# A gating mixer's norm: gamma and beta taken behind the spatial product

## The chip, the cores and the metric

The kernel runs on one core of a Trainium2 chip. The time is the device time of one execution in microseconds (us); the version before takes 566.77 us, the median of 3 runs (566.43 to 567.15). The engines have short names here, as in the profile: PE is the matrix engine (PEld its weight loads), DVE the vector engine, ACT the scalar engine, POOL the GpSimd engine, SP the engine that issues nearly all DMAs. Each engine takes its own instructions strictly in the order in which they were issued, and waits for the others by semaphores.

## The reference

A trunk of two layers over 256 tokens of width 1024. Layer 0 mixes tokens with a gated MLP, layer 1 with attention; each is followed by a gated FFN with a short convolution, and each sub-layer by a residual and a LayerNorm. Only the mixer of layer 0 changes:

```python
def chunked_gmlp(x, w_in, ln_g, ln_b, w_s, b_s, w_out):
    z = gelu(x @ w_in)
    u, v = split(z, 2)                       # 1024 columns each
    v = layer_norm(v, ln_g, ln_b)            # (v - mean) * rstd * gamma + beta, per token
    v = v.reshape(B, 2, 128, 8, 128)         # 2 chunks of 128 tokens, 8 groups of 128 channels
    w = tril(w_s)                            # per group a 128 x 128 causal matrix
    sv = einsum('gts,bnsgc->bntgc', w, v) + b_s.T[..., None]
    return (u * sv.reshape(B, S, 1024)) @ w_out
```

All data are float32. Gamma and beta differ per channel c; the weights w mix the tokens s of a chunk; b_s is one number per group and token t. Since the spatial product sums over tokens and gamma does not depend on them, sum over s of w[t,s] (n[s,c] gamma[c] + beta[c]) = gamma[c] (w n)[t,c] + beta[c] (sum over s of w[t,s]), where n is the normalized v.

## The kernel before, in words

Every large matrix product is made from three: operands are split into a high part (rounded to a faster 4-byte type) and a low remainder, and high x high, high x low and low x high are summed in PSUM. The weights come in chunks of 1 MB (`stream`, 128 x 2048 in the two tiles `raw`). For each half of a chunk ACT rounds the high part (`whi<-raw`, line 353) and DVE subtracts it to get the low one (`wlo<-raw,whi`, line 359); ten pairs `whi`/`wlo` are in use in turn. A chunk is loaded when the chunk five places ahead of it has been used. Chunks 0 to 3 are `a_v` (the columns of w_in for v), 4 to 7 `a_u` (for u), 8 to 11 `a_out`, then `f_up0` and so on. Chunk 4 lands in the tile that later holds x, hence `x<-in_a_u` and `wlo<-x,whi`.

The mixer, `gmlp` (lines 696 to 755), goes through four stages on PE:

1. v = x @ a_v, token-major: two token tiles t, each of two PSUM banks of 512 columns, eight steps k of the contraction.
2. For each of 8 groups g of u, channel-major: `cols_apart` with 16 matmuls (8 steps, a 512-column one with `whi` and a 256-column one with `wlo`); ACT copies half of the bank (`uparts<-bank`), DVE adds the other (`ff<-bank,uparts`), ACT applies the GELU.
3. Meanwhile v gets its GELU (ACT, `ff<-bank`), its statistics (`stats`, DVE: `BATCH_NORM_STATS2`, aggregate, add of epsilon; POOL: a power of -1/2 on one column, line 557) and its norm (`scaled`): per token tile two instructions of 512 columns, (v - mean) * gamma, and four of 256, (. * rstd) + beta, with gamma and beta as rows in the tile `lnrow`, copied to all partitions by a DMA.
4. `spatial(g)`: PE multiplies v's group with the masked weights `ws` into a PSUM half bank (`twos<-ff`, plain float32), DVE adds the bias row of the group (`ff<-twos,ff`), multiplies by u (`ff<-ff`), and the product is split into high (ACT, `rr<-ff`) and low (DVE, `rr<-ff,rr`). Then a_out contracts over the groups, k = g.

`load_mixer` loads the transposed spatial weights (`wsT`), masks them on POOL (`affine_select`, line 496) and loads the bias rows (`bs`). `load_rest` loads x again in token layout, `lncol` (gammas and betas as columns, for later norms) and the convolution's constants (`convc`).

The order of instructions on each engine is not the order of the code. Everything is recorded in a `Plan` with an estimated duration; `Plan.emit` (lines 124 to 220) walks through time with these estimates and picks on each engine the waiting operation with the earliest due time. PE's bulk matmuls keep their order, the `fill` ones (spatial products, transposes) slip in when they are estimated to be ready. What comes out is a fixed sequence per engine; a row that waits on the chip holds up everything behind it on its engine. `after` (line 76) only holds an issue back until a named one has been issued.

## Time and profile before

| | |
|---|---|
| median of 3 runs | 566.77 us (566.43 to 567.15) |
| the profiled execution's own time | 566.5 us |
| its span in the trace | 564.7 us |
| PE busy | 555.1 us, 98% of the span |
| DVE busy | 467.9 us, 83% |
| ACT busy | 363.9 us, 64% |
| POOL busy | 11.2 us, 2% (18 instructions) |
| mean granted PE clock | 0.996 |

The span runs from the first instruction to the last; 1.8 us of the execution lie outside it. In rows of the timeline the first number is the start in us from the span's start, the second the time from the first to the last instruction of the row, then engine, line, operation, output<-inputs by the program's names, shapes and a count; in brackets how long the engine had been idle before and what released it. "PE bank L341 <- DVE rr L359" in the list of waits reads: PE's instruction of line 341 that writes a PSUM bank waited for DVE's instruction of line 359 that writes `rr`; then total us, count, longest. Rows of a table of windows give, for a stretch of the span, the busy us and the count of instructions of PE, PEld, DVE, ACT and POOL, the granted clock (1.00 is full), the DMA engines' share and GB/s.

### The profile page before, as it was taken

How to read it: one execution, taken by the hardware profiler on the slowest of the kernel's cores; microseconds unless marked ns; L12 is line 12 of the kernel's file. 1: busy time of each engine (PE TensorE's matmuls, PEld its weight loads, DVE VectorE, ACT ScalarE, POOL GpSimd, SP SyncE). 2: the span in 40 equal slices, each digit the busy share in tenths (PEclk: the TensorE clock that was granted, in tenths of full speed). 3: DMA queues.
4: the chain of work that ended last, by engine and by line, in shares of the span. 5: the costliest groups of instructions: out<-in, count | busy, mean ns of one | idle time of the engine just before them, and what ended most of it. 6: DMA issues, size and time to landing. Idle time of an engine off the chain costs nothing.

```text
span 564.7 us, 8191 instructions
## 1 busy us (share of the span) xinstructions
PE 555.1 (98%) x3041; PEld 472.8 (84%) x3041; DVE 467.9 (83%) x886; ACT 363.9 (64%) x660; POOL 11.2 (2%) x18
## 2 busy tenths in 40 slices
PE   8999999999999999999999999999999999999994
PEld 6888788888888888888888887788888888888884
DVE  6599989999999897568868888589998999997426
ACT  6557568767777684535678888288777776885200
POOL 0010010000000000001000000000000000000001
PEclk9999999999999999999999999999999999999998
DMA  8977536454545559671655553506456455667202
GB/s 304 386 288 272 195 135 225 169 203 171 203 176 199 178 202 334 236 261 34 242 199 187 187 192 146 224 9 237 187 199 257 157 209 168 223 225 265 103 0 75
DMA packets 19856, 110.97 MB, mean 197 GB/s; under 512 B 2326, under 2 KB 5608, under 8 KB 7656
## 3 DMA queue, kind: packets, MB, share of 16 engines
q1 hardware_dynamic: 19672, 110.18, 54.0%
q8 instruction: 24, 0.39, 0.3%
q10 hardware_dynamic: 144, 0.26, 0.1%
q14 instruction: 16, 0.13, 0.1%
HBM read 109.36 MB, written 1.07 MB: 196 GB/s over the span
## 4 chain that ended last, share of the span: by engine, by line
PE 93%; DVE 5%; DMA 1%; issue 1%; ACT 0%; DVEq 0%
PE twos L341 52%; PE bank L341 38%; DVE wlo L359 2%; PE bank L347 1%; PE twos L347 1%; DMA raw<-in_a_out 1%; PE twos L974 1%; DVE ff L359 1%; DVE stat L551 1%; DVE ff L363 0%; DVE x L363 0%; DVE rr L359 0%; ACT whi L353 0%; ACT ff L353 0%; DVE stat L554 0%
## 5 line engine op out<-in xcount | busy, mean ns | idle before, releaser
L359 DVE TENSOR_TENSOR wlo<-raw,whi 128x1024 fp32r<-128x1024 f32 (+1 forms) x210 | 227.0, 1102 | 35.3 <-ACT whi L353 34.9
L353 ACT ACTIVATE whi<-raw 128x1024 fp32r<-128x1024 f32 (+1 forms) x210 | 193.7, 954 | 61.9 <-DMA raw<-in_f_dn 23.4
L341 PE MATMUL twos<-xt,whi 128*128 128x512 f32 x640 | 222.2, 394 | 0.0
L341 PE MATMUL twos<-xt,wlo 128*128 128x256 f32 x640 | 177.3, 277 | 0.0
L341 PEld LDWEIGHTS twos<-xt,whi 128*128 128x128 f32 x640 | 120.0, 188 | 27.8
L341 PE MATMUL bank<-whi,rr 128*128 128x512 f32 x432 | 135.7, 391 | 0.5 <-DVE rr L359 0.5
L341 PEld LDWEIGHTS twos<-xt,wlo 128*128 128x128 f32 x640 | 120.1, 188 | 0.1
L341 PEld LDWEIGHTS bank<-whi,rr 128*128 128x128 f32 x432 | 81.0, 188 | 18.2 <-DVE rr L359 0.9
L341 PE MATMUL bank<-wlo,rr 128*128 128x512 f32 x216 | 84.1, 389 | 0.0
L363 DVE SCALAR_TENSOR_TENSOR ff<-ff,convc 128x255 f32<-128x255 f32 (+1 forms) x160 | 70.3, 477 | 1.1 <-ACT ff L353 0.9
L341 PE MATMUL bank<-xt,whi 128*128 128x512 f32 x192 | 69.0, 401 | 0.0
L341 PE MATMUL bank<-xt,wlo 128*128 128x256 f32 x192 | 53.8, 280 | 0.0
L353 ACT ACTIVATE ff<-twos 128x512 f32<-128x512 f32 (+1 forms) x56 | 30.8, 565 | 33.6 <-PE twos L341 30.8
L353 ACT ACTIVATE ff<-ff,convc 128x256 f32<-128x256 f32 x80 | 46.5, 593 | 3.1 <-DVE ff L359 2.6
L341 PEld LDWEIGHTS bank<-wlo,rr 128*128 128x128 f32 x216 | 40.6, 188 | 8.1
L341 PEld LDWEIGHTS bank<-xt,whi 128*128 128x128 f32 x192 | 36.1, 188 | 8.8 <-issue 0.5
L341 PE MATMUL twos<-whi,xt 128*128 128x512 f32 x128 | 42.1, 396 | 0.0
L359 DVE TENSOR_TENSOR ff<-twos,ff 128x512 f32<-128x512 f32 (+1 forms) x48 | 30.7, 642 | 8.9 <-ACT ff L353 8.5
L341 PEld LDWEIGHTS bank<-xt,wlo 128*128 128x128 f32 x192 | 36.3, 189 | 0.1
L353 ACT ACTIVATE ff<-bank,lncol 128x128 f32<-128x128 f32 x48 | 18.8, 460 | 25.9 <-PE bank L347 25.8
L341 PEld LDWEIGHTS twos<-whi,xt 128*128 128x128 f32 x128 | 24.1, 188 | 4.7
L363 DVE SCALAR_TENSOR_TENSOR x<-x,bank 128x512 f32<-128x512 f32 x16 | 10.9, 684 | 20.6 <-PE bank L341 20.6
(86 smaller groups left out, 499.7 us busy)
## 6 DMA issues: line engine op xcount, KB each, us to landing
raw<-in_f_up SPq DMA_DIRECT2D x44, 1024.0 KB, 4.8
raw<-in_f_dn SPq DMA_DIRECT2D x22, 1024.0 KB, 4.9
raw<-in_b_qk SPq DMA_DIRECT2D x8, 1024.0 KB, 4.8
lnrow<-in_lnrow SPq DMA_DIRECT2D x5, 1024.0 KB, 6.1
raw<-in_a_out SPq DMA_DIRECT2D x4, 1024.0 KB, 5.1
raw<-in_b_v SPq DMA_DIRECT2D x4, 1024.0 KB, 4.8
raw<-in_b_o SPq DMA_DIRECT2D x4, 1024.0 KB, 5.0
raw<-in_a_v SPq DMA_DIRECT2D x7, 512.0 KB, 5.6
```

Source lines behind the costliest of these rows:

```text
L341: nc.tensor.matmul(o, l, x, start=start, stop=stop)
L347: nc.tensor.transpose(o, x, ident.ap)
L353: return plan.op("act", ns, lambda: nc.scalar.activation(o, x, func, **kw), r, w, table=table)
L359: dve(70 + 1.04 * flat(x), lambda: nc.vector.tensor_tensor(o, x, y, op=op), r, w)
L363: lambda: nc.vector.scalar_tensor_tensor(o, x, s, y, op0=op0, op1=op1), r, w)
L551: dve(70 + 1.04 * n, lambda j=j, o=o, n=n: nc.vector.bn_stats(s[:, j, :], x[:, o:o + n]), [(r, range(o // S, (o + n) // S))], [(st, [("st" ...
L974: nc.tensor.matmul(banks[-1], zeros[:, :P], zeros, start=True, stop=True)
```

## The change

v is only normalized, (v - mean) * rstd, by two `tensor_scalar` instructions of 512 columns per token tile. The rows gamma and beta of this norm are no longer loaded. Behind the spatial product a `scalar_tensor_tensor` takes the place of the addition: product times gamma (a column of `lncol`, which gains 16 columns) plus a table per group. This table, `bs`, is the bias plus beta[c] times the row sum of the masked weights, and is built on the chip:

- the spatial weights are loaded a second time, untransposed (`ws`, 0.5 MB), into the first half of the one tile that rotates through `lnrow`; POOL masks them; DVE sums over s (`tensor_reduce`, 128 x 1024 to 128 x 8);
- a DMA writes the 4 KB of sums to a scratch in DRAM, a second one reads them back to all 128 partitions (0.5 MB into the tile's second half);
- POOL multiplies, group by group, the sums (every eighth element) by beta's column, and adds the result to the bias rows: 16 instructions of 128 columns.

`lncol` is loaded in `load_mixer` now. The core of the diff:

```diff
     def load_mixer():
         wsT, bs = place("ff", 3072, SUB), place("ff", 4096, SUB)
+        natural = rowring.new()
+        nv = natural.ap[:, :SUB].rearrange("p (g s) -> p g s", g=GROUPS)
+        load(nv, a["ws"], [(natural, ["ws"])]).after = loads[5]
         load(wsT.ap, a["wsT"], [wsT])
+        load(lncol.ap, a["lncol"], [lncol])
         v = wsT.ap.rearrange("p (g t) -> p g t", g=GROUPS)
         plan.op("pool", 1100, lambda: nc.gpsimd.affine_select(
             v, v, pattern=[[0, GROUPS], [1, P]], compare_op=ALU.is_ge, fill=0.0, base=0,
             channel_multiplier=-1), [wsT], [wsT])
-        load(bs.ap, bass.AP(tensor=a["bs"].tensor, offset=a["bs"].offset, ap=[[0, P], [1, GROUPS * P]]), [bs])
-        return (wsT, v), (bs, bs.ap.rearrange("p (g t) -> p g t", g=GROUPS))
+        bv = bs.ap.rearrange("p (g t) -> p g t", g=GROUPS)
+        load(bs.ap, bass.AP(tensor=a["bs"].tensor, offset=a["bs"].offset, ap=[[0, P], [1, GROUPS * P]]),
+             [(bs, QUART), (bs, range(4, GROUPS))])
+        plan.op("pool", 1600, lambda: nc.gpsimd.affine_select(
+            nv, nv, pattern=[[0, GROUPS], [-1, P]], compare_op=ALU.is_ge, fill=0.0, base=0,
+            channel_multiplier=1), [(natural, ["ws"])], [(natural, ["ws"])])
+        sums, scr = Buf(sb.tile([P, GROUPS], F32, name="sums")), Buf(dram.tile([P, GROUPS], F32, name="sumscr"))
+        dve(1140, lambda: nc.vector.tensor_reduce(out=sums.ap, in_=nv, axis=mybir.AxisListType.X, op=ALU.add),
+            [(natural, ["ws"])], [sums])
+        load(scr.ap, sums.ap, [scr], [sums], nbytes=4096)
+        everywhere = natural.ap[:, SUB:]
+        load(everywhere, bass.AP(tensor=scr.ap.tensor, offset=scr.ap.offset, ap=[[0, P], [1, GROUPS * P]]),
+             [(natural, ["sums"])], [scr])
+        ev = everywhere.rearrange("p (t g) -> p g t", g=GROUPS)
+        for g in range(GROUPS):
+            plan.op("pool", 500, lambda g=g: nc.gpsimd.tensor_scalar_mul(
+                ev[:, g, :], ev[:, g, :], lncol.ap[:, 7 * KT + g:7 * KT + g + 1]),
+                [(natural, ["sums"]), lncol], [(natural, [g])])
+            plan.op("pool", 600, lambda g=g: nc.gpsimd.tensor_tensor(
+                bv[:, g, :], ev[:, g, :], bv[:, g, :], op=ALU.add), [(natural, [g]), (bs, [g])], [(bs, [g])])
+        return (wsT, v), (bs, bv)
...
             if (k, t) == (3, NT - 1):
-                rows = ln_rows(0)
                 ws, bs = load_mixer()
...
-                scaled(vt, vt.ap, st, mean, rstd, rows)
+                for o in (0, HALF):
+                    parts = range(o // S, (o + HALF) // S)
+                    ts(vt.ap[:, o:o + HALF], vt.ap[:, o:o + HALF], mean, rstd, ALU.subtract, ALU.mult,
+                       [(vt, parts), (st, ["mv", "rstd"])], [(vt, parts)])
...
-            tt(y3, b.ap[:, :S].rearrange("p (c t) -> p c t", c=NT), bs[1][:, g:g + 1, :].to_broadcast([P, NT, P]),
-               ALU.add, [b, bs[0]], [y])
+            stt(y3, b.ap[:, :S].rearrange("p (c t) -> p c t", c=NT), lncol.ap[:, 6 * KT + g:6 * KT + g + 1],
+                bs[1][:, g:g + 1, :].to_broadcast([P, NT, P]), ALU.mult, ALU.add, [b, (bs[0], [g]), lncol], [y])
```

The planner sees other operations and other estimates, so sequences move on every engine. In the rows below a name is a tile and its number, `[waits ...]` the semaphores, by engine or DMA queue, on which the row waits.

On DVE, at the passage from v's product to u's (raw_85, raw_86 and x are weight chunks, whi/wlo their high and low halves; stat holds the norm's statistics, lnrow_89 the untransposed spatial weights). Before:

```order
L359 TENSOR_TENSOR wlo_82<-raw_86,whi_72 128x1024 [waits DMAHW3_49,Activation_49]
L551 BN_STATS stat_90<-ff 128x6 [waits Activation_49]
L359 TENSOR_TENSOR wlo_83<-x,whi_73 128x1024 [waits DMAHW4_49]
L359 TENSOR_TENSOR wlo_84<-x,whi_74 128x1024 [waits Activation_49]
L359 TENSOR_TENSOR wlo_75<-raw_85,whi_65 128x1024 [waits DVE_49,DMAHW5_49,PE_49,Activation_49]
```

And now:

```order
L359 TENSOR_TENSOR wlo_82<-raw_86,whi_72 128x1024 [waits DMAHW3_49,Activation_49]
L510 TENSOR_REDUCE sums<-lnrow_89 128x8 [waits Pool_49]
L573 BN_STATS stat_90<-ff 128x6 [waits Activation_49]
L359 TENSOR_TENSOR wlo_83<-x,whi_73 128x1024 [waits DMAHW5_49]
L359 TENSOR_TENSOR wlo_84<-x,whi_74 128x1024 [waits Activation_49]
```

The sum over the weights stands between wlo_82 and the first statistics, ahead of the low halves of u's first chunk, and waits for POOL.

On SP, the DMA issues of the same stretch (sumscr is the scratch in DRAM). Before:

```order
L377 DMA x<-in_a_u 128x2048 [waits DMAHW4_49]
L377 DMA raw_85<-in_a_u 128x2048 [waits DMAHW1_49,DMAHW0_49,DVE_49]
L377 DMA lnrow_89<-in_lnrow 128x2048
L377 DMA ff<-in_wsT 128x1024 [waits DMAHW7_49]
L377 DMA ff<-in_bs 128x1024
L377 DMA lncol<-in_lncol 128x48
L377 DMA raw_86<-in_a_u 128x2048 [waits DMAHW3_49,DMAHW2_49,DVE_49]
L377 DMA raw_85<-in_a_u 128x2048 [waits DMAHW5_49,DVE_49]
```

And now:

```order
L377 DMA ff<-in_wsT 128x1024 [waits DMAHW4_49]
L377 DMA x<-in_a_u 128x2048
L377 DMA raw_85<-in_a_u 128x2048 [waits DMAHW1_49,DMAHW0_49,DVE_49]
L377 DMA lnrow_89<-in_ws 128x1024 [waits DMAHW7_49]
L377 DMA sumscr<-sums 128x8 [waits DVE_49]
L377 DMA ff<-in_bs 128x1024
L377 DMA lncol<-in_lncol 128x64 [waits DMAHW2_49]
L377 DMA convc<-in_convc 128x352 [waits DMAHW3_49]
L377 DMA raw_86<-in_a_u 128x2048 [waits DMAHW4_49,Activation_49]
L377 DMA raw_85<-in_a_u 128x2048 [waits DMAHW6_49,DMAHW5_49,DVE_49]
L377 DMA lnrow_89<-sumscr 128x1024 [waits DMAHW0_49]
```

wsT has moved ahead of u's first chunk, the 1 MB of gamma and beta is replaced by the 0.5 MB of untransposed weights, and the write of the sums, which waits for DVE, stands ahead of the bias and of u's third and fourth chunk (the last two raw rows).

On DVE, at the first spatial product (twos is its PSUM half bank, bank the one of u):

```order
L359 TENSOR_TENSOR wlo_80<-raw_85,whi_70 128x1024 [waits Activation_49]
L359 TENSOR_TENSOR ff<-bank_108,uparts_116 128x256 [waits Activation_49]
L363 SCALAR_TENSOR_TENSOR ff<-twos_104,lncol,ff 128x256 [waits DMAHW1_49,DMAHW2_49,PE_49,Pool_49]
L366 TENSOR_SCALAR ff<-ff,stat_90 128x512
L359 TENSOR_TENSOR ff<-ff 128x256 [waits DVE_49]
L366 TENSOR_SCALAR ff<-ff,stat_91 128x512
```

Before, the addition that stood in the place of the third row waited for at most one DMA queue and PE, and none of them for POOL; now each of the eight also waits for the POOL addition that completes its group's table.

More of the change, by code (lines that the diff above doesn't have):

```diff
@@ L450, in trunk_kernel @@
     ident, nhalf = const("ident", P), const("nhalf", 1)
-    lncol, convc = const("lncol", 6 * KT), const("convc", DEPTH * 2 * FT * 4)
+    lncol, convc = const("lncol", 8 * KT), const("convc", DEPTH * 2 * FT * 4)
     plan.op("pool", 400, lambda: make_identity(nc, ident.ap), (), [ident])
@@ L486, in ln_rows @@
         src = a["lnrow"]
-        o = load(b.ap, bass.AP(tensor=src.tensor, offset=src.offset + i * 2 * D, ap=[[0, P], [1, 2 * D]]), [b])
-        if i == 0:
-            o.after = loads[5]
+        load(b.ap, bass.AP(tensor=src.tensor, offset=src.offset + i * 2 * D, ap=[[0, P], [1, 2 * D]]), [b])
         return b, b.ap.rearrange("p (a d) -> p a d", a=2)
@@ L504, in load_rest @@
             load(xtok[t].ap, a["x"][:, t, :], [(xtok[t], QUART)])
-        load(lncol.ap, a["lncol"], [lncol])
         load(convc.ap, a["convc"], [convc])
@@ L577, in ln_back @@
         step = KT // len(waits)
-        lc = lncol.ap.rearrange("p (i a k) -> p i a k", i=3, a=2)
+        lc = lncol.ap.rearrange("p (i a k) -> p i a k", i=4, a=2)
         x = r.ap
@@ L1011, in _layout @@
         "b_o": by_rows(np.asarray(i["b_w_o"])[0]),
+        "ws": f(np.asarray(i["a_w_s"])[0].transpose(1, 0, 2)),
         "wsT": f(np.asarray(i["a_w_s"])[0].transpose(2, 0, 1).reshape(P, -1)),
@@ L1027, in _layout @@
     g["lnrow"] = f(np.stack([np.stack(p) for p in lns]))
-    g["lncol"] = f(np.stack([np.stack(p) for p in lns[1:4]]).reshape(3 * 2 * KT, P).T)
+    g["lncol"] = f(np.stack([np.stack(p) for p in lns[1:4] + lns[:1]]).reshape(4 * 2 * KT, P).T)
     cw, cb = np.asarray(i["f_conv_w"]), np.asarray(i["f_conv_b"])
```

## The prediction

> **What bounds the kernel now.** I read the page's totals and its chain first, then PE's list of waits, then the table of windows over the mixer, then the timeline of each engine there.
>
> ```profile
> PE 555.1 (98%) x3041; PEld 472.8 (84%) x3041; DVE 467.9 (83%) x886; ACT 363.9 (64%) x660; POOL 11.2 (2%) x18
> PE 93%; DVE 5%; DMA 1%; issue 1%; ACT 0%; DVEq 0%
> ...
> PE twos L974 <- DVE nhalf L453: 1.5, 1, 1.5
> PE bank L341 <- DVE rr L359: 0.5, 1, 0.5
> ...
> 30.00:40.00 10.00, 9.86 (x59) 8.56 (x58) 10.00 (x19) 5.67 (x9) 1.71 (x2) 1.00 0.73 247
> 40.00:50.00 10.00, 10.00 (x63) 8.93 (x63) 9.89 (x17) 6.41 (x11) 0.00 (x0) 1.00 0.66 248
> 50.00:60.00 10.00, 10.00 (x56) 8.61 (x55) 10.00 (x25) 7.35 (x14) 0.00 (x0) 1.00 0.71 270
> 60.00:70.00 10.00, 9.50 (x43) 7.53 (x42) 9.31 (x17) 4.81 (x10) 0.00 (x0) 1.00 0.62 216
> ```
>
> PE is the bound, and in the whole span it waits for another engine twice: 1.5 us at the start, 0.5 us once in a_out. Two things follow. The change adds and removes no work on PE, so at best it gains that half microsecond. And every new wait of PE stays in the time, since no later wait exists that could take it up. But in the mixer (30 to 64 us) DVE is full (fourth and fifth numbers of the windows: DVE's 10.00, 9.89, 10.00), and the 0.5 us is DVE being late. So two questions decide: does the change make PE wait where it did not, and does DVE come out earlier or later at the end of the mixer?
>
> **First place: the sum over the weights.** These rows give the passage from v to u.
>
> ```profile
> 13.46 0.42 SPq L377 DMA_DIRECT2D x<-in_a_u  x1
> 17.26 0.33 SPq L377 DMA_DIRECT2D raw<-in_a_u  x1
> 17.64 0.43 SPq L377 DMA_DIRECT2D lnrow<-in_lnrow  x1
> 18.11 0.44 SPq L377 DMA_DIRECT2D ff<-in_wsT  x1
> 20.96 0.33 SPq L377 DMA_DIRECT2D raw<-in_a_u  x1
> ...
> 21.05 1.06 ACT L353 ACTIVATE whi<-x 128x1024 fp32r<-128x1024 f32 x1 [1.39 <-DMA x<-in_a_u]
> 31.52 1.06 ACT L353 ACTIVATE whi<-raw 128x1024 fp32r<-128x1024 f32 x1 [0.16 <-DMA raw<-in_a_u]
> 27.70 1.61 POOL L496 TENSOR_SCALAR_AFFINE_SELECT ff<-ff 128x1024 f32<-128x1024 f32 x1 [26.30 <-DMA ff<-in_wsT]
> ...
> 25.40 0.69 DVE L551 BATCH_NORM_STATS2 stat<-ff 128x6 f32<-128x512 f32 x1 [4.47 <-ACT ff L353]
> 26.01 1.21 DVE L359 TENSOR_TENSOR wlo<-x,whi 128x1024 fp32r<-128x1024 f32 x1
> 27.14 1.22 DVE L359 TENSOR_TENSOR wlo<-x,whi 128x1024 fp32r<-128x1024 f32 x1
> 28.27 2.11 DVE L359 TENSOR_TENSOR wlo<-raw,whi 128x1024 fp32r<-128x1024 f32 x1
> 28.20 0.28 PE L341 MATMUL bank<-xt,wlo 128*128 128x256 f32 x1
> 28.54 0.28 PE L341 MATMUL bank<-xt,wlo 128*128 128x256 f32 x1
> ```
>
> The DMAs land in the order of their issue, behind one another: between the landing of x (21.05) and of wsT (27.70) lie raw, lnrow and wsT, 2.5 MB in 6.65 us, 2.66 us per MB; bias, lncol and the next raw (1.5 MB) then land at 31.52, at 2.55 us per MB. In the new order of SP wsT stands ahead of x, and 0.5 MB of ws in the place of 1 MB of lnrow. Counted from x's landing less its own 2.66 (18.4): wsT 19.7, x 22.4, raw 25.0, ws 26.4.
>
> Then the new chain, each link waiting for the one before. POOL masks ws: the row of wsT's mask says 1.61, but POOL started 0.66 before DVE's instruction ended (27.14 + 1.22 = 28.36) and finished 0.95 after it. So it takes 1.0 to 1.6; DVE stands still here, I take 1.15: 27.55. DVE's sum over 1024 columns has no row; the nearest are DVE's 1024-column subtractions, 1.22 long and 1.13 apart: 28.7. Then, behind it in DVE's order, the first statistics (25.40 to 26.01, 0.61): 29.3, and the low half of u's first chunk, 1.21: 30.5. Before, this low half started at 26.01 and ended at 27.2; PE took it up at 28.20, with 1.0 us to spare. It starts 3.3 later now, so **PE waits 2.3 to 2.4 us at 28.2**, where it never waited. The 4.47 us in which DVE stood idle ahead of 25.40 are no cover, since ws has not landed by then. With mask, sum and landing at their ends (1.0 and 1.6; 1.13 and 1.3; half a microsecond either way) the wait is between 1.5 and 3.4.
>
> Everything on DVE behind that row moves along. SP too is held: its issue of the sums' write waits for the sum, and behind it stand bias, lncol, convc and u's third chunk, which is issued at about 30.8 (28.8 and four issues of 0.45 to 0.7) in the place of 20.96.
>
> ```profile
> raw<-in_a_u SPq DMA_DIRECT2D x1, 1024.0 KB, 4.7
> ```
>
> An idle queue lands it 4.7 us later, at 35.6 in the place of 31.52. PE needs it for group 4. A group is eight steps of some 0.35 (28.20 to 28.54), so group 4 began at 39.2 at the earliest before (28 and four times 2.8) and begins later now: ACT's two halves (1.06 each) and DVE's two (1.13 each) fit, without a cost of their own. The second mask now falls beside nothing, and wsT's earlier one (19.7) beside low halves that PE needs 2 us later: nothing there.
>
> **Second place: DVE up to the end of the mixer.** Its ledger, from these groups (line and form, busy us, mean ns) and rows:
>
> ```profile
> L363 DVE SCALAR_TENSOR_TENSOR ff<-ff,stat,lnrow 128x256 f32<-128x256 f32 x8 | 3.7, 476 | 0.0
> L359 DVE TENSOR_TENSOR ff<-twos,ff 128x256 f32<-128x256 f32 x8 | 3.2, 416 | 0.1
> L363 DVE SCALAR_TENSOR_TENSOR ff<-ff,stat,lnrow 128x512 f32<-128x512 f32 x4 | 2.9, 742 | 0.0
> 71.92 1.00 DVE L366 TENSOR_SCALAR x<-x,stat 128x512 f32<-128x512 f32 x2 [0.44 <-POOL stat L557]
> 63.22 0.75 DVE L359 TENSOR_TENSOR rr<-ff,rr 128x256 fp32r<-128x256 f32 x2
> 63.69 0.73 PE L341 MATMUL bank<-whi,rr 128*128 128x512 f32 x2 [0.50 <-DVE rr L359]
> ```
>
> - later start: +3.3;
> - wsT's mask no longer stretches a subtraction (2.11 against 1.22): -0.9;
> - the norm: 12 instructions of 3.7 + 2.9 = 6.6 us go, four of 0.5 come; successive rows overlap by about 0.08 (1.22 long, 1.13 apart), so -5.6 + 1.7 = -3.9;
> - eight additions become scalar-and-tensor instructions, 476 against 416 ns: +0.5;
> - new waits on DVE, for the power on POOL and for the first table: 0.5 to 1.3, I take +0.8.
>
> That is -0.2, and the 16 instructions of POOL are still to come. None of their kind has a row. The nearest:
>
> ```profile
> 1.11 0.29 POOL masks.py:199 TENSOR_SCALAR_AFFINE_SELECT ident<-ident 128x128 f32<-128x128 f32 x1
> 255.87 0.55 POOL L557 TENSOR_TENSOR stat<-stat,nhalf 128x1 f32<-128x1 f32 x1 [175.22 <-DVE stat L556]
> 265.54 1.39 POOL L557 TENSOR_TENSOR stat<-stat,nhalf 128x1 f32<-128x1 f32 x1 [9.12 <-DVE stat L556]
> 265.31 1.22 DVE L359 TENSOR_TENSOR wlo<-raw,whi 128x1024 fp32r<-128x1024 f32 x1
> ```
>
> 128 columns in one operation took 0.29, a power on one column 0.55: 4.6 to 8.8 us for 16. They run from about 40 on (the sums, 0.5 MB, land behind u's fourth chunk) beside a full DVE, and the two get in each other's way: the power took 1.39 in the place of 0.55 because it began beside a subtraction, and wsT's mask cost the subtraction behind it 0.9 of the 0.95 in which POOL still ran. So I count on DVE what POOL holds while DVE has a two-input instruction from SBUF in hand. If all of POOL falls into DVE's waits it is 0; if all of it is paid, 4.6 to 8.8. The row nearest in width gives 0.29; with a second input in half of them 0.3, and about two thirds on DVE's busy stretches: 16 x 0.3 x 0.67 = +3.2.
>
> The Trainium skill, page "SBUF — State Buffer", section "Who interferes with whom", has it as a rule: a DVE instruction with two SBUF inputs and a GpSimd instruction that reads SBUF exclude each other for the whole instruction. Both rows above agree (1.39, 2.11). By the rule without my two thirds the term is 4.8.
>
> DVE's end in the mixer is thus 3.0 later (from -0.2 to +8.6), its last low halves start at 66.2 in the place of 63.22, and PE, which waited for them at 63.69, goes on 3.0 later. PE on its own, with the 2.4 of the first place, some 0.3 at the first spatial products (both tiles' first halves must be normalized now, not a quarter) and without the old 0.5, would be 2.2 later. The later one counts: **+3.0 us**. Past the mixer the moved rows (transposes and attention's small products shift by a few places) meet a PE that waits for nobody: 0, with 0.3 either way.
>
> **The rivals.**
>
> *POOL's turn-taking rules.* Each table needs its POOL addition, each addition the one ahead, and POOL gets in only between DVE's long instructions. With 0.55 each and every one paid, the ledger is -0.2 + 8.8 = 8.6; DVE's own waits for a table overlap part. Middle of 4.6 (all 16 paid at 0.3) and 8.6: +6.6, 573.4. For it: DVE without a gap from 30 to 60. Against it: the row of 0.29.
>
> *Not slower: the sum fits into DVE's gap.* DVE idles 4.47 us ahead of 25.40. If ws landed by about 24.0 (mask 1.15, sum 1.15 until 26.3, less the 1.0 that PE has to spare) nothing would reach PE, DVE would start 0.9 late at most, and with light POOL instructions (0 to 1 us in all) the ledger ends below 0: PE loses its old wait, -0.5 to +0.5, 566.3 to 567.3. The point is the landing of ws: it needs transfers that overtake one another. The rows of 21.05, 27.70 and 31.52 speak against it.
>
> *PE's clock drops at the new wait.*
>
> ```profile
> 556.00:558.00 2.00, 1.22 (x11) 1.02 (x9) 0.71 (x2) 0.00 (x0) 0.00 (x0) 1.00 0.21 70
> 558.00:560.00 2.00, 0.00 (x0) 0.00 (x0) 1.93 (x6) 0.00 (x0) 0.92 (x1) 1.00 0.00 0
> 560.00:562.00 2.00, 0.00 (x0) 0.00 (x0) 1.50 (x4) 0.00 (x0) 0.00 (x0) 0.51 0.36 120
> ```
>
> After PE's last work (557.2) the granted clock stays at 1.00 until 560 and is half (0.51) behind it: 2.8 us of idling did not lower it. A wait of 2.4 stays below, one of 3.4 would not. If it fell for as long again, PE would lose half of some 3 us, +1.5 on top of +4: 572.3. The Trainium skill, page "TensorE: Matmul & The Clock Gate", Part 1, sets the window of idling at some 3.4 us; by that too the clock holds here.
>
> **How the numbers follow.** Executions of this kernel scatter by 0.36 either way, so anything within 0.2% (1.1 us) counts as no change. The profiled execution took 566.5, 0.3 below the median; I add to the median: 566.8 + 3.0 = 569.8. Chances: the forecast 0.60 (from +1.3, PE's own 2.2 with the first wait at its low end of 1.5, to +4.6); POOL's turns, above that, 0.18; the clock 0.05; the sum in the gap, or DVE's savings taking up nearly all, 0.14, of which nearly all within 0.2%; something else that makes it faster 0.03. The range leaves out the lowest case and the heaviest of POOL: 567.5 to 573.3. Slower 0.83, same 0.13, faster 0.04.
>
> **What would show it.** DVE's sum between 27.5 and 29, idle ahead of it for over 5 us; PE's wait for `wlo` of about 2.4 at 28.2; u's third chunk landing past 35; 16 short POOL rows between 40 and 56 whose length grows with DVE's row beside them; DVE's last `rr` at about 66. I am wrong if PE's list shows no wait at 28, if POOL's rows leave DVE's alone (+2.2 then), or if PE waits past the mixer.

## The result, and the profile after

The change takes 571.66 us (median, 570.98 to 572.01) against 566.68 us of the kernel before in the same series (566.43 to 567.15): a ratio of 1.0092, 95% interval 1.0079 to 1.0104. It is slower by 5.0 us; the forecast was 569.8, 3.0 slower, within 567.5 to 573.3. The profiled execution took 571.66, its span is 569.9 us against 564.7, so 5.2 us are to be explained.

The page's totals, then PE's list of waits in the profile of the change (total us, count, longest):

```profile
PE 555.4 (97%) x3041; PEld 472.4 (83%) x3041; DVE 466.8 (82%) x879; ACT 360.8 (63%) x660; POOL 29.8 (5%) x35
...
PE bank L341 <- DVE wlo L359: 3.1, 1, 3.1
PE twos L341 <- DVE ff L366: 2.7, 3, 1.6
PE twos L998 <- DVE nhalf L453: 1.5, 1, 1.5
```

PE does the same work as before (555.4 us against 555.1). It has four new waits, 3.1 + 2.7 = 5.8 us, and has lost the old one of 0.5 in a_out: 5.3 us, nearly the whole difference of the spans. The waits lie at three places.

**First, the low half of u's first chunk.** Rows of the timeline of POOL, DVE and PE (start, length, operation, what it waited for):

```profile
26.86 1.09 POOL L506 TENSOR_SCALAR_AFFINE_SELECT lnrow<-lnrow 128x1024 f32<-128x1024 f32 x1 [4.21 <-DMA lnrow<-in_ws]
27.98 1.22 DVE L510 TENSOR_REDUCE sums<-lnrow 128x8 f32<-128x1024 f32 x1 [6.29 <-POOL lnrow L506]
29.12 0.69 DVE L573 BATCH_NORM_STATS2 stat<-ff 128x6 f32<-128x512 f32 x1
29.72 2.34 DVE L359 TENSOR_TENSOR wlo<-x,whi 128x1024 fp32r<-128x1024 f32 x2
30.99 0.39 PE L341 MATMUL bank<-xt,wlo 128*128 128x256 f32 x1 [3.05 <-DVE wlo L359]
```

ws lands at 26.9, the mask takes 1.1, the sum 1.1 (27.98 to 29.12), the statistics 0.6, the low half 1.2; PE stands still from 27.94 to 30.99.

**Second, the late third chunk of u.** SP's issues, ACT's and DVE's rows and PE's first spatial products, with three stretches of the table of windows (the last three numbers are the clock, the share of the DMA engines and GB/s):

```profile
30.56 0.43 SPq L377 DMA_DIRECT2D convc<-in_convc  x1
31.09 3.61 SPq L377 DMA_DIRECT2D raw<-in_a_u  x2
...
31.00:33.00 2.00, 2.00 (x12) 1.78 (x13) 2.00 (x2) 0.00 (x0) 0.00 (x0) 1.00 0.95 217
33.00:35.00 2.00, 2.00 (x14) 1.75 (x13) 2.00 (x4) 0.38 (x1) 0.00 (x0) 1.00 0.77 211
35.00:37.00 2.00, 2.00 (x13) 1.76 (x12) 1.89 (x7) 0.00 (x0) 0.49 (x1) 1.00 1.02 412
...
38.35 2.00 ACT L353 ACTIVATE whi<-raw 128x1024 fp32r<-128x1024 f32 x2 [4.12 <-DMA raw<-in_a_u]
39.45 1.23 DVE L359 TENSOR_TENSOR wlo<-raw,whi 128x1024 fp32r<-128x1024 f32 x1 [1.81 <-ACT whi L353]
40.59 0.54 DVE L366 TENSOR_SCALAR ff<-ff,stat 128x512 f32<-128x512 f32 x1
41.18 1.83 PE L341 MATMUL twos<-ff 128*128 128x128 f32 x14 [1.60 <-DVE ff L366]
```

The chunk is issued at 31.09, behind the sums' write, bias, lncol and convc, and lands at 38.3, 7.2 us later. Its low half (39.45) stands ahead of the second token tile's norm in DVE's order (40.59), and for that norm the first spatial products wait: 1.6 us. From 31 to 35 the DMA engines are 95% and 77% busy and yet move only half of what they move from 35 on (217 and 211 GB/s against 412). That is some 0.86 MB, and bias, lncol and convc are 0.74 MB, so most of the chunk came behind 35 (an estimate from these rows); in run 2 below they are not in front. lncol and convc have short rows (256 and 1408 bytes); that this is why so little moves is argued, not tested.

**Third, the table on POOL.** DVE, POOL and PE from 42 on:

```profile
42.51 2.35 DVE L359 TENSOR_TENSOR wlo<-raw,whi 128x1024 fp32r<-128x1024 f32 x2
42.53 3.80 POOL L518 TENSOR_SCALAR lnrow<-lnrow,lncol 128x128 f32<-128x128 f32 x2 [4.86 <-DMA lnrow<-sumscr]
46.17 1.07 POOL L521 TENSOR_TENSOR ff<-lnrow,ff 128x128 f32<-128x128 f32 x2
46.78 0.48 DVE L363 SCALAR_TENSOR_TENSOR ff<-twos,lncol,ff 128x256 f32<-128x256 f32 x1 [1.58 <-POOL ff L521]
47.77 0.49 PE L341 MATMUL twos<-ff 128*128 128x128 f32 x2 [0.59 <-DVE ff L366]
48.78 0.49 PE L341 MATMUL twos<-ff 128*128 128x128 f32 x2 [0.52 <-DVE ff L366]
...
53.85 3.12 DVE L359 TENSOR_TENSOR wlo<-raw,whi 128x1024 fp32r<-128x1024 f32 x2
67.73 0.74 DVE L359 TENSOR_TENSOR rr<-ff,rr 128x256 fp32r<-128x256 f32 x2
```

POOL's first multiplication (3.04 of the 3.80 us of its row) begins 0.02 us behind a pair of subtractions on DVE and does not get through before both are over (42.51 to 44.86). DVE then waits 1.58 for the first table, and PE twice for what stands behind that wait, 0.59 and 0.52. DVE's last low halves (67.73) start 4.5 us later than before, but PE, 5.3 later by its own waits, does not wait for them.

### The profile page after: what moved, and what is told of

Read it like the earlier page. It is cut to its first block, busy times and chain, and to the rows that moved or that the text cites. A ratio compares the mean times of both kernels' runs of the same rounds, so it can differ in the third digit from the quotient of the medians.

```text
span 569.9 us, 8222 instructions
## 1 busy us (share of the span) xinstructions
PE 555.4 (97%) x3041; PEld 472.4 (83%) x3041; DVE 466.8 (82%) x879; ACT 360.8 (63%) x660; POOL 29.8 (5%) x35
## 4 chain that ended last, share of the span: by engine, by line
PE 90%; DMA 5%; DVE 2%; issue 1%; POOL 0%; ACT 0%; SPq 0%; DVEq 0%; POOLq 0%
PE twos L341 51%; PE bank L341 37%; DMA raw<-in_a_v 2%; DMA lnrow<-in_ws 2%; DMA lnrow<-sumscr 1%; PE bank L347 1%; DVE wlo L359 1%; PE twos L347 1%; DVE x L363 0%; ACT whi L353 0%; SPq L377 0%; DVE stat L573 0%; POOL lnrow L506 0%; POOL lnrow L518 0%; DVE ff L366 0%
## 5 line engine op out<-in xcount | busy, mean ns | idle before, releaser
L363 DVE SCALAR_TENSOR_TENSOR ff<-ff,convc 128x254 f32<-128x254 f32 (+1 forms) x160 | 69.5, 477 | 0.7 <-ACT ff L353 0.3
L359 DVE TENSOR_TENSOR ff<-twos,ff 128x512 f32<-128x512 f32 x40 | 27.6, 690 | 11.6 <-ACT ff L353 11.6
L579 POOL TENSOR_TENSOR stat<-stat,nhalf 128x1 f32<-128x1 f32 x10 | 8.3, 837 | 506.3 <-DVE stat L578 506.3
L353 ACT ACTIVATE ff<-ff 128x256 f32<-128x256 f32 x52 | 20.9, 409 | 12.4 <-DVE rr L359 8.7
```

The costliest lines, as they stand in the source:

```text
L353: return plan.op("act", ns, lambda: nc.scalar.activation(o, x, func, **kw), r, w, table=table)
L359: dve(70 + 1.04 * flat(x), lambda: nc.vector.tensor_tensor(o, x, y, op=op), r, w)
L363: lambda: nc.vector.scalar_tensor_tensor(o, x, s, y, op0=op0, op1=op1), r, w)
L579: plan.op("pool", 465, lambda: nc.gpsimd.tensor_tensor(rstd, ve, nhalf.ap, op=ALU.pow), [(st, ["ve"]), nhalf], [(st, ["rstd"])])
```

## The experiments

Each kernel is the change with the edit shown. Runs 1 to 4, 5 to 8 and 9 to 12 are three series; each was compared with the kernel before in its own series (566.12, 566.05 and 566.14 us), and gains are taken from the ratios, 0.001 being 0.57 us.

The theory after the result: the table costs, not the norm, and it costs by three separate waits of PE, each of which can be taken away by its own edit. The rivals: the new norm or the sharing of SBUF by POOL and DVE costs; and, from run 3 on, the halved clock behind PE's first wait costs.

**1. Without the table.** No second load of ws, no mask, sum, round trip or POOL work; beta's part is left out, the new norm and the multiplication by gamma stay.

```diff
-        natural = rowring.new()
-        load(nv, a["ws"], [(natural, ["ws"])]).after = loads[5]
...
-        dve(1140, lambda: nc.vector.tensor_reduce(out=sums.ap, ...
-        load(scr.ap, sums.ap, [scr], [sums], nbytes=4096)
...
```

> The moved norm alone: gamma and the plain normalization as in the change, but the table of beta times the row sums is left out (the second load of the weights, its mask, the sum, the two small transfers, POOL's 16 instructions), so beta's part is missing from the output. Theory A (all of the loss comes from building the table): PE's three new waits are gone, and DVE, some 3 us lighter, is no longer late at a_out: 566.2 (565.8 to 566.7). Rival C (the moved norm itself costs, since the first spatial products need halves of v instead of quarters, and DVE's scalar form is longer): over 567.2, with a wait of PE for the tensor_scalar rows.

Measured: 565.93 us, ratio 0.9998 (0.9989 to 1.0008). The list of PE's waits has one row left, that of the start, and DVE waits for PE in a_out:

```profile
PE twos L978 <- DVE nhalf L453: 1.5, 1, 1.5
...
68.14 0.69 DVE L363 SCALAR_TENSOR_TENSOR x<-x,bank 128x512 f32<-128x512 f32 x1 [0.87 <-PE bank L341]
```

So all of the loss comes from building the table, to within the half microsecond of the interval. The lighter norm itself relieves DVE (it now waits for PE) and takes PE's old 0.5 away, too little to be measured.

**2. The sum held back** until DVE has made the low halves of u's first chunk.

```diff
-        dve(1140, lambda: nc.vector.tensor_reduce(out=sums.ap, ...
+        summed = dve(1140, lambda: nc.vector.tensor_reduce(out=sums.ap, ...
+        summed.after = chunks[EARLY][1][1].wr[0]
```

> The sum over the weights held back on DVE by three rows, behind both low halves of u's first chunk; nothing else is moved but SP's issues around it (the bias and the constants no longer stand behind the write of the sums, u's third chunk still does). Theory A (a chain of late landings: each takes PE's time only as far as the next does not): the wait of 3.1 at 28 is gone, u's third chunk lands at about 35 and holds the normalization so that PE waits 1 to 2 at the first spatial products, and POOL's table is late for DVE, another 1 to 2: 569 to 570.5. Rival A2 (the three waits simply add): 571.7 - 3.1 = 568.6 or less. Rival B (POOL and DVE excluding each other is what costs): 571.7 within 0.5.

Measured: 569.36 us, 1.0050 (1.0035 to 1.0065). The wait of 3.1 is gone; PE comes to the spatial products that much earlier and waits there instead:

```profile
38.74 1.83 PE L341 MATMUL twos<-ff 128*128 128x128 f32 x14 [2.12 <-DVE ff L366]
45.61 0.49 PE L341 MATMUL twos<-ff 128*128 128x128 f32 x2 [0.80 <-DVE ff L366]
46.58 0.49 PE L341 MATMUL twos<-ff 128*128 128x128 f32 x2 [0.48 <-DVE ff L366]
```

2.4 us of the loss came back (1.0092 less 1.0050): the place of one DVE instruction is worth almost half of it. The profile also speaks to the late third chunk. Here bias, lncol and convc were issued at 18 to 19.5, the chunk at 30.82 with only the sums' write in front, and it landed at 35.91: 5.1 us in the place of 7.2, close to the 4.7 of an idle queue. So the transfers in front of it made up most of the delay in the change.

**3. The sums' write held back** on SP, behind the issue of u's third chunk.

```diff
-        load(scr.ap, sums.ap, [scr], [sums], nbytes=4096)
+        load(scr.ap, sums.ap, [scr], [sums], nbytes=4096).after = loads[6]
```

> The sum stays where the change put it, but SP issues the write of the sums behind u's third chunk instead of ahead of it and of the constants. Theory A: the wait of 3.1 at 28 stays, the 1.6 at the first spatial products goes (third chunk landed by 32), the 1.1 behind POOL's table becomes 0.5 to 1: 569.7 to 570.6. If instead the 1.6 stays, the held SP queue is not its cause. Rival B: 571.7 within 0.5.

Measured: 570.32 us, 1.0066 (1.0050 to 1.0083). The waits of 1.6 and 1.1 at the spatial products are gone, as expected, but in this profile for another reason too: PE's clock was halved behind the first wait, and PE came late. One window (the clock is the third number from the end) and PE's rows there:

```profile
32.00:34.00 2.00, 2.00 (x8) 1.71 (x7) 2.00 (x3) 0.00 (x0) 0.00 (x0) 0.50 0.00 0
...
31.52 0.52 PE L341 MATMUL bank<-xt,wlo 128*128 128x256 f32 x1 [2.75 <-DVE wlo L359]
31.84 0.63 PE L341 MATMUL bank<-xt,whi 128*128 128x512 f32 x1
```

A step of two products took 0.64 us in the place of 0.35. The 24 steps up to the first spatial product took 9.78 us against 8.21 in the profile of the change, where a longer wait (3.05) had not lowered the clock: 1.6 us. This raised a second question, whether half speed is part of what the change costs. The profiled execution is not typical, though: it was the slowest of the four (571.13), with a mean clock of 0.992; the other three had 0.997 or 0.998 and took 569.88 to 570.61. The median says little about half speed.

**4. Both held back**, the edits of runs 2 and 3 together.

> Both holds: the sum behind the low halves of u's first chunk, its write behind u's third chunk; the table is still built by POOL and beside DVE as in the change. Theory A: the first two waits of PE are gone, the one behind POOL's table is left with 0.5 to 1.7: 566.7 to 568.2. Rival B: no better than 570.

Measured: 568.55 us, 1.0042 (1.0027 to 1.0057), a little above the range of the theory. PE waits 2.4 us in three pieces at the first spatial products (0.96 for the norm of both tiles, 0.93 and 0.48 behind the table), 0.2 more there, and 0.5 at the start. DVE still waits for POOL:

```profile
PE twos L341 <- DVE ff L366: 2.4, 3, 1.0
...
DVE ff L363 <- POOL ff L522: 1.7, 1, 1.7
DVE sums L510 <- POOL lnrow L506: 1.0, 1, 1.0
```

The two holds give back 2.8 us (1.0092 less 1.0042); 2.5 us above the kernel without a table (0.9998) remain.

**5. Both, and the table on DVE**: one `scalar_tensor_tensor` per group in the place of POOL's two instructions.

```diff
-            plan.op("pool", 500, lambda g=g: nc.gpsimd.tensor_scalar_mul(
-                ev[:, g, :], ev[:, g, :], lncol.ap[:, 7 * KT + g:7 * KT + g + 1]), ...
-            plan.op("pool", 600, lambda g=g: nc.gpsimd.tensor_tensor(
-                bv[:, g, :], ev[:, g, :], bv[:, g, :], op=ALU.add), ...
+            stt(bv[:, g, :], ev[:, g, :], lncol.ap[:, 7 * KT + g:7 * KT + g + 1], bv[:, g, :], ALU.mult, ALU.add,
+                [(natural, ["sums"]), lncol, (bs, [g])], [(bs, [g])])
```

> The two holds of the run both, and in addition the table of each group is built by one scalar_tensor_tensor on DVE in the place of a multiplication and an addition on POOL: 8 instructions of 128 columns on DVE, none on POOL. Theory (PE pays for three separate waits, and of these the table's comes from POOL): DVE's wait for POOL's table (1.65 in the run both) goes, 8 short instructions of some 0.25 to 0.4 come onto DVE, PE's waits at the first spatial products (2.4 in three there) fall to about 1.0 to 1.5: 567.1 to 567.6 against 568.55 of the run both. Rival (the wait for the table is really the wait for the sums to come back by DMA, so that DVE only waits in POOL's place): PE's waits stay at 2.4 and the time at 568.3 to 568.8.

Measured: 568.26 us, 1.0040 (1.0027 to 1.0053), executions from 567.52 to 569.35. This misses the range of the theory: two of the five executions lie in it, the median is that of the run before. Yet DVE's wait for POOL and PE's two behind it are gone. PE's waits, and DVE and ACT at the first transposes behind a_out:

```profile
PE bank L347 <- DVE x L366: 1.1, 1, 1.1
PE twos L341 <- DVE ff L366: 0.9, 1, 0.9
PE bank L341 <- DVE rr L359: 0.4, 1, 0.4
...
73.18 2.19 ACT L353 ACTIVATE whi<-raw 128x512 fp32r<-128x512 f32 x4 [6.75 <-DMA raw<-in_f_up]
73.84 0.69 DVE L359 TENSOR_TENSOR wlo<-raw,whi 128x512 fp32r<-128x512 f32 x1 [2.08 <-ACT whi L353]
75.05 1.11 PE L347 MATMUL bank<-ident,x 128*128 128x128 f32 x8 [1.09 <-DVE x L366]
```

PE comes to the transposes 1.0 us sooner than in run 4 (73.96 against 74.93) and loses 1.09 there: in DVE's order a low half of f_up0 stands ahead of the norm that they need, and its chunk landed at 73.2 (at 69.2 in run 4). In this execution the wait moved past the mixer; it took 569.23, so the rows do not speak for the two executions near 567.5, which were not profiled.

**6. Sums that lie next to each other**: POOL's multiplication reads 128 adjacent values, not every eighth (beta's part is then taken from the wrong sums).

```diff
-        ev = everywhere.rearrange("p (t g) -> p g t", g=GROUPS)
+        ev = everywhere.rearrange("p (g t) -> p g t", g=GROUPS)
```

> The change with one edit: POOL's multiplications read and write 128 sums that lie next to each other, not every eighth one. The table then belongs to other tokens (beta's part of the mixer is computed from the wrong sums); every engine's order of instructions is that of the change. Theory (the 0.91 us of a lone multiplication, against 0.57 of a lone addition, is its step of eight elements): the lone multiplication takes 0.4 to 0.6, POOL's rows as a whole get 2 to 4 us shorter, DVE's wait for the first table falls from 1.6 to about 1.2, PE's waits for the first products by as much: 571.0 to 571.4. Rival (the step costs nothing, 0.91 is what such an instruction takes): rows and time stay, 571.5 to 571.9.

Measured: 571.29 us, 1.0090 (1.0076 to 1.0104). POOL's rows:

```profile
42.88 3.01 POOL L518 TENSOR_SCALAR lnrow<-lnrow,lncol 128x128 f32<-128x128 f32 x2 [3.22 <-DMA lnrow<-sumscr]
49.42 1.19 POOL L518 TENSOR_SCALAR lnrow<-lnrow,lncol 128x128 f32<-128x128 f32 x2
```

A pair of multiplications now takes down to 1.19, 0.6 each; with the step of eight elements no pair took less than 2.18 in the change's profile, and 1.81 was the least in any run, 0.9 each. The 16 instructions together take 14.4 us against 18.4. The step was the reason for the 0.91 us of a multiplication, but the time does not show it: 571.29 lies in the theory's range and yet cannot be told from the change (its ratio was 1.0092). Nor could the profiled execution show it: PE had waited 4.77 us at the first place, with half the clock behind it, and came to the spatial products without a wait.

**7. The sum done twice.**

```diff
-        dve(1140, lambda: nc.vector.tensor_reduce(...),
+        dve(1140, lambda: [nc.vector.tensor_reduce(...) for _ in range(2)],
```

> The change with its sum over the weights done twice in a row on DVE; the order is otherwise that of the change. Theory (the first wait of PE is DVE's lateness and nothing takes it up): PE's wait for wlo goes from 3.1 to 4.2, the write of the sums and u's third chunk move by the same, so that the later waits stay as they are: 571.66 + 1.15 = 572.8 (572.6 to 573.1). With the clock falling behind the longer wait, as it fell behind 2.75 us in the run write_behind, some 1.6 more: 574 to 574.8, and a granted clock below 0.8 in the windows behind the wait. Rival (later slack takes a part up): below 572.3.

Measured: 572.95 us, 1.0126 (1.0110 to 1.0141), within the theory's range, but the single executions go from 571.67 to 573.80. The profiled one was the lowest, and it had both a longer wait (4.86) and half the clock behind it, which by the theory should have given 574 or more:

```profile
32.82 0.58 PE L341 MATMUL bank<-xt,wlo 128*128 128x256 f32 x1 [4.86 <-DVE wlo L359]
...
32.00:34.00 2.00, 1.18 (x4) 1.09 (x5) 2.00 (x3) 0.00 (x0) 0.00 (x0) 0.59 0.74 212
```

There PE had no wait left at the spatial products. So the number was met without the reason given for it: what PE loses at the first place it does not lose again at the second and third. Nor is the longer wait the second sum's alone. The untransposed weights landed at 27.44 here and at 26.86 in the change, and in the profiles that keep the change's order the first wait follows this landing: 3.05 and 3.01 us at 26.86 (the change, run 9), 3.65 at 27.63 (run 8), 4.77 at 28.84 (run 6).

**8. The table computed but not used**: POOL's results go beside the table, so nothing waits for POOL; beta's part is left out.

```diff
             plan.op("pool", 600, lambda g=g: nc.gpsimd.tensor_tensor(
-                bv[:, g, :], ev[:, g, :], bv[:, g, :], op=ALU.add), ...
+                ev[:, g, :], ev[:, g, :], bv[:, g, :], op=ALU.add), ...
```

> The change with one edit: POOL's additions write their results beside the table and not into it, so that the instructions behind the spatial products use the plain bias and wait for no POOL instruction; beta's part of the mixer is left out. All of POOL's 16 instructions still run, and every engine's order is that of the change. Theory (POOL costs by being waited for): DVE's wait for POOL (1.6) goes, PE's two waits of 0.59 and 0.52 behind it go: 571.66 - 1.1 = 570.5 (570.2 to 570.8). Rival (POOL costs by holding DVE's instructions up while both use SBUF): DVE's stretched rows stay and with them the time, 571.3 to 571.8.

Measured: 571.46 us, 1.0092 (1.0078 to 1.0106). The theory (570.5) missed, and the number lies in the rival's range. The profile does not speak for the rival either: the wait for POOL is gone, but PE had waited 3.65 at the first place and gone on at half clock (24 steps in 10.74 us, 2.5 more than at full speed), so it reached the spatial products only at 42.50 and without a wait, where what the table costs could not show.

Runs 9 to 12 shared a chip. Three of them keep PE at work in the first wait: the first product of u, whose high half is there early, is computed ten times more into the bank that it then overwrites, 2.3 us of work that nobody needs (`again` is 10 at the first step of u's first group and 0 elsewhere).

```diff
         def emit():
+            for _ in range(again):
+                nc.tensor.matmul(seq[0][0], seq[0][1], seq[0][2], start=True, stop=True)
```

**9. The change once more**, beside them.

> The change itself, unaltered, beside the three runs with ten repeated products, so that all four share a chip. Theory: its time is made of chains that end at about the same place, PE's first wait (with half speed behind it in some executions) and the late third chunk with the table; so its time stays near 571.5 (570.8 to 572.0) and its granted clock differs between executions (0.991 to 0.997) without the time following it. Rival: the time follows the clock, executions at 0.991 take 1.5 to 2 us longer than those at 0.996 or more.

Measured: 572.53 us, 1.0112 (1.0095 to 1.0129), executions from 570.41 to 574.19 at mean clocks of 0.990 to 0.994. The median is above the theory's range and the scatter wider than expected. The time does not follow the clock: the lowest time had 0.992, the two at 0.994 took 572.53 and 572.98. No execution here had 0.996, but in the first series of the change 570.98 had 0.991 and 571.66 and 572.01 had 0.996; the rival that the time follows the clock falls. The profile shows half clock and no wait of 1.6 at the first spatial products:

```profile
30.98 0.58 PE L341 MATMUL bank<-xt,wlo 128*128 128x256 f32 x1 [3.01 <-DVE wlo L359]
49.04 0.49 PE L341 MATMUL twos<-ff 128*128 128x128 f32 x2 [0.48 <-DVE ff L366]
...
32.00:34.00 2.00, 2.00 (x8) 1.71 (x8) 2.00 (x3) 0.00 (x0) 0.00 (x0) 0.50 0.80 129
```

Its 24 steps took 10.97 us, 2.8 more than in the first profile of the change, but its span is only 0.4 longer (570.3 against 569.9).

**10. The change with the ten products.**

> The change with ten more products on PE: the first product of u (high half, 512 columns), whose operands are there 3 us before the low half, is computed ten times over into the same bank before it counts, 2.3 us of work in the place of idling; every engine's order is otherwise that of the change. Theory: PE's wait at 28 shrinks from 3.1 to 3.7 down to 0.7 to 1.5, the clock stays at 1.00 behind it in every execution, but PE then meets the late third chunk and the late table at the first spatial products, as in the profile of the change (1.6, 0.6, 0.5): 571.0 to 571.7, as the change. Rival (the half clock is what the change costs): 569.3 to 570.3.

Measured: 570.92 us, 1.0093 (1.0077 to 1.0109), 569.92 to 572.97, mean clocks of 0.996 to 0.998 in all six executions. The clock held, as both expected. The median falls between the two ranges, 0.1 below the theory's and 0.6 above the rival's; it lies 1.6 below run 9, but the executions and the intervals overlap, so a gain is not established. The profile shows the chain that comes next:

```profile
30.68 0.39 PE L343 MATMUL bank<-xt,wlo 128*128 128x256 f32 x1 [0.35 <-DVE wlo L361]
39.81 1.83 PE L343 MATMUL twos<-ff 128*128 128x128 f32 x14 [0.54 <-DVE ff L368]
46.95 0.49 PE L343 MATMUL twos<-ff 128*128 128x128 f32 x2 [0.48 <-DVE ff L368]
```

**11. Run 3 with the ten products.**

> The run write_behind (the sums' write issued behind u's third chunk) with the same ten repeated products. There the third chunk is in time, so that the first wait and the clock behind it stand alone. Theory (half speed after the wait cost that run some 1.6 us): no window below 0.95 of granted clock behind the wait, PE's wait at 28 down to 0.5 to 1.3, 568.5 to 569.3 against 570.32. Rival (the clock had no part): 570.0 to 570.6.

Measured: 570.34 us, 1.0068 (1.0055 to 1.0081); run 3 had 1.0066. The theory (568.5 to 569.3) missed, the number is the rival's. The clock held, so that the 1.6 us of half speed in run 3's profile are not there, but PE then found the table unfinished:

```profile
32.00:34.00 2.00, 2.00 (x13) 1.76 (x12) 2.00 (x3) 0.00 (x0) 0.00 (x0) 1.00 0.00 0
...
46.46 0.49 PE L343 MATMUL twos<-ff 128*128 128x128 f32 x2 [0.84 <-DVE ff L368]
47.43 0.49 PE L343 MATMUL twos<-ff 128*128 128x128 f32 x2 [0.48 <-DVE ff L368]
```

In the profile of run 3 the slow stretch had hidden these two waits. And three of run 3's four executions had a clock of 0.997 or more, so there was little half speed in its median to save.

**12. Run 8 with the ten products.**

> The run table_unused (POOL's results go beside the table; beta's part is left out) with the same ten repeated products, so that PE does not arrive late from half speed and hide what the table costs. Theory (DVE's wait for POOL's first table is paid where PE comes in time): 0.8 to 1.1 below the run warm, 570.0 to 570.6, with PE's wait of 1.6 for the normalized v still there and those behind it gone. Rival (POOL costs only by holding DVE up): within 0.3 of the run warm.

Measured: 571.11 us, 1.0093 (1.0074 to 1.0112), 569.56 to 573.93, 0.2 above run 10. The number is the rival's. The profiled execution was the slowest and does not settle it: no wait behind the table is left, but u's third chunk came at 38.47 (36.97 in the profile of run 10), and a chunk of f_up0 was late at the transposes:

```profile
41.30 1.83 PE L343 MATMUL twos<-ff 128*128 128x128 f32 x14 [1.57 <-DVE ff L368]
71.13 0.69 DVE L361 TENSOR_TENSOR wlo<-raw,whi 128x512 fp32r<-128x512 f32 x1 [3.13 <-ACT whi L355]
78.97 1.16 PE L349 MATMUL bank<-ident,x 128*128 128x128 f32 x8 [2.13 <-DVE x L368]
```

**The books of PE.** In each profile: PE's waits beyond the 1.5 us at the start, plus half speed (the time of the 24 steps from PE's first low-half product of u to the first spatial product, less 8.2), plus 2.3 for the ten products where they are, less the old 0.5; beside it what the span is longer than 564.7.

| run | new waits | half speed | sum less 0.5 | span longer by |
|---|---|---|---|---|
| the change | 5.8 | 0.0 | 5.3 | 5.2 |
| the change once more | 3.7 | 2.8 | 6.0 | 5.6 |
| without the table | 0.0 | not read | -0.5 | -0.7 |
| sum held back | 3.6 | 0.0 | 3.1 | 3.2 |
| write held back | 3.2 | 1.6 | 4.3 | 4.6 |
| both | 3.1 | 0.0 | 2.6 | 1.8 |
| both, table on DVE | 2.4 | 0.0 | 1.9 | 2.8 |
| adjacent sums | 5.0 | 1.9 | 6.4 | 5.4 |
| sum twice | 4.9 | 1.3 | 5.7 | 5.1 |
| table unused | 3.9 | 2.5 | 5.9 | 5.1 |
| ten products | 1.9 | 0.0 | 3.7 | 3.5 |
| write held back, ten products | 2.2 | 0.0 | 4.0 | 3.9 |
| table unused, ten products | 4.8 | 0.0 | 6.6 | 7.5 |

The sums agree with the spans within 0.4 in seven rows and within 1.0 in all. What follows: the first wait, half speed behind it, the third chunk and the table are chains that end at about the same place, and what PE does not lose to one of them it loses in part to the next. Together they are the table's price, 5.3 us (1.0092 less 0.9998); holding the sum back is worth 2.4, holding the write back 1.5, both 2.8. How much POOL's part costs by itself stays open: three kernels that took the wait for POOL away (runs 5, 8, 12) did not become measurably faster, each with another wait or half speed in its place.

No kernel here beats the one before: the best that keeps the computation, run 5, is 1.0040 of it.

## Why the prediction was right or wrong

- **Slower, through PE's new waits:** right. PE's work is unchanged, no slack took the waits up, and without the table the time is that of before. The time was 1.9 us above the forecast, inside its range, and that is in part luck: the term that was to decide, DVE's end, did not, and PE's own sum came out at 5.3 in the place of 2.2.
- **The first wait, 2.4:** right place and mechanism, measured 3.05. Mask (1.1), sum (1.1) and statistics (0.6) were as priced; ws landed 0.5 later (26.9 against 26.4) and PE arrived 0.3 earlier (27.94). Both lie within the bounds that were given (up to 3.4).
- **"PE needs it for group 4 ... without a cost of their own":** this step failed. The issue (31.09) was as forecast, the landing was not: 38.3, not 35.6. The 4.7 us were those of an idle queue, and the queue was not idle: bias, lncol and convc are issued right in front of the chunk. The working had counted their issues and not their transfers; with them out of the way (run 2) the landing took 5.1. The path was another one too: not group 4 needed the chunk first, but its low half stood in DVE's order ahead of the second token tile's norm (39.45, 40.59). It cost 1.6 us at the first spatial products, where 0.3 was set for another reason.
- **POOL, +3.2 on DVE:** the cost came by another way. 16 instructions of 0.3 were assumed; the least that one took in the change was 0.52 for an addition and 0.91 for a multiplication. But DVE lost little by sharing: 0.2, 0.8 and 0.2 in three stretched rows, 1.2 in all. It was POOL that stood back, 3.04 us for its first multiplication. DVE paid by waiting 1.58 for the first table, and PE 1.1 behind that. The Trainium skill, page "SBUF — State Buffer", section "Who interferes with whom", says that the two exclude each other for the whole instruction; the row of 42.53 agrees, and it shows more: with two subtractions back to back on DVE, POOL came in behind the second only. That is not the rule: the multiplication that began at 50.30 took 2.22 us and was over at 52.52, before the second of the two subtractions beside it (53.20).
- **"The later one counts: +3.0" (DVE's end):** this step failed. DVE's last low halves came 4.5 later (67.73; 3.0 was forecast), but PE, delayed by its own 5.3, came later still and did not wait for them. PE's own sum, set at 2.2, was the one that counted; it lacked 0.7 at the first wait (3.05 less 2.4), 1.3 at the third chunk (1.60 less the 0.3 that was set) and 1.1 at the table (0.59 + 0.52): 2.2 + 0.7 + 1.3 + 1.1 = 5.3.
- **The clock rival (0.05):** its mechanism exists and its bound was wrong. "A wait of 2.4 stays below, one of 3.4 would not" took the 2.8 us of one row as a threshold. Waits of 2.75 and 3.01 were followed by half speed, one of 3.05 was not. It cost up to 2.8 us of slower steps, but little in the end as far as these profiles show (a span 0.4 longer in run 9), since PE then came too late to meet the waits behind. The Trainium skill, page "TensorE: Matmul & The Clock Gate", Part 1, describes a free-running window of some 3.4 us, with half speed after an idle one; that the outcome differs behind 3.01 and 3.05 us would fit a phase that differs from run to run, but the 2.75 and 3.01 us with half speed behind them are both shorter than that window, so its length is not borne out here.
- **POOL's turns (+6.6):** not what happened, though 574.19 in one execution of run 9 shows that such times occur; that execution was not profiled, and its cause is open. **The sum in DVE's gap:** no; ws landed at 26.9, not 24.0.
- **Past the mixer "a PE that waits for nobody":** true in the profile of the change, not in all runs. In two profiles (runs 5 and 12) PE waited 1.1 and 2.1 at the first transposes, when a chunk of f_up0 came late.

## What to carry to other kernels

Where one engine is the bound, an added side computation is not priced by its own work but by the in-order queues in which it stands: here one DVE instruction of 1.1 us ahead of what PE needs, and one tiny write on SP ahead of a weight chunk, are worth 2.8 of 5.3 us. A transfer's landing is to be counted from everything that is issued in front of it, not from the time that it takes in an idle queue. And when several chains are late by about the same, removing one wait shows the next one: the waits of a profile add up to about its time, but they do not add up as gains: taking away the first (3.05) brought 2.4, the first and the second (4.65) brought 2.8, and taking away the wait for POOL brought nothing that could be measured.

## What the runs showed of the hardware

- Half speed of PE does not follow the length of a wait alone: behind 2.75 and 3.01 us of waiting a step of two products took 0.64 us, behind 3.05 it took 0.35, in the same instruction order for the last two. Behind 3.65, 4.77 and 4.86 it was half speed in each profile. In run 9 the clock fell at 30.2 (1.00 up to 30.0, 0.68 from 30.0 to 30.5), 2.2 us into the wait, and stayed at half until 37.0, 6.0 us after PE had gone on. With ten products that nobody needs in the wait, the clock stayed at 1.00 in the windows behind it in all three profiles.
- A multiplication of 128 columns on POOL took 0.9 with a step of eight elements and 0.6 with adjacent ones.
- Two subtractions back to back on DVE (2.35 us, from 42.51) kept a POOL instruction out for both; another one, from 50.30, got through before the second had ended.
- For 4 us the DMA engines were 95% and 77% busy with 217 and 211 GB/s, then full with 412.
- The change widened the scatter: 570.41 to 574.19 over nine executions, 565.62 to 567.15 for the kernel before in all series. In the seven profiles with the change's order on SP, the untransposed weights landed at 26.55 to 28.84, and PE's first wait hangs on this landing; that it makes the scatter is likely, not shown, since most executions were not profiled.
